# Last step of the experts: outputs and loads in column blocks, sums of the norm by block, and unread products

## The chip, the core and the metric

The kernel runs on one core of one Trainium2 chip. The metric is the time of one execution on the device in microseconds (us), the median over runs. PE is TensorE, PEld its weight loads, DVE is VectorE, ACT is ScalarE, POOL is GpSimd; SP issues the DMAs.

## What is computed

A transformer block, then a second block that ends in a mixture of 64 experts, for 256 tokens of width 1024, all in float32. What matters here is the end: each token goes through 6 of 64 experts, their weighted sum is added to the residual, and a norm over the 1024 outputs closes the block.

```python
def expert_block(xs):
    tok, g, e = xs
    xb = x_pad[tok]
    hb = jax.nn.silu(xb @ w_exp_gate[e]) * (xb @ w_exp_up[e])
    return (hb @ w_exp_down[e]) * g[:, None]
...
x = x + gate_f * moe_ffn(h, ...)
...
def rms_norm_2(x, gain):
    xf = x.astype(jnp.float32)
    y = xf * lax.rsqrt(jnp.mean(xf * xf, axis=-1, keepdims=True) + NORM_EPS)
    return (y * gain.astype(jnp.float32)).astype(x.dtype)
```

## The kernel before

The experts are sorted by load and worked off in 24 steps of 128 token slots each: steps of two experts with 64 slots or of four experts with 32 slots. The last step has four experts of 32 slots, so a product of one expert fills a quarter of the array's columns (128x32 weights) and one quarter of the partitions of its PSUM bank. Each expert brings three matrices of 1 MB: gate `eg` and up `eu` (1024x256) and down `ed` (256x1024). They are read once, so this part of the program is a long row of loads.

All loads are issued by SP in one order, set by `plan_step`; a load starts when a slot of SBUF is free, and up to eight are under way, since each waits for the landing of the one eight places earlier. In the last step `eu` comes in two halves of k and `ed` in two halves of output columns, `j` outside and experts inside.

A step runs so. `hidden(p)`: for gate and then up, k from 0 to 7 outside and experts inside, products accumulate in one bank; ACT and DVE make silu(gate) x up. `hidden_T` turns that around, `slots_T` makes `ST` (which slot belongs to which token) and `gcol` (the slots' gate weights). `down(p, c)`: for output half c, two k outside and experts inside, 32x512 products in one bank; DVE multiplies by `gcol` and `gate_f`; ACT and DVE split the result into `y_hi` and `y_lo`. `combine(p, c)` multiplies by `ST` and accumulates in four banks `moe[t][c]` (token half t, output half c) that hold the residual from the start (`seed`, where PE first runs four identity products over whole banks).

In the last step half 1 is not split: DVE leaves it as `yv` in float32. Then the norm. `half_norm` takes half 0: `measure` squares and sums a bank on ACT, `gained` multiplies it by the norm's gain on DVE. `norm` measures half 1, adds up, raises to the power -1/2 on POOL, scales (half 0 on ACT, half 1 on DVE) and stores four pieces of 128x512. PE, ACT and DVE work through their instructions in the order in which they are written; ACT and DVE wait for each other where both read one bank. Line numbers of the end:

```python
down(p, 0)
down(p, 1)
combine(p, 0)
half_norm()
combine(p, 1)
norm()
```

Of the kernel before, what the change touches and what calls it, by code (L numbers as in the profile page):

```python
# [10 lines left out]
F32 = mybir.dt.float32  # L11
# [4 lines left out]
OP = mybir.AluOpType  # L16
# [351 lines left out]
def tile_block(ctx: ExitStack, tc: tile.TileContext, a: dict, out: bass.AP, taps=None):  # L368
# [289 lines left out]
    steps = [step for g in groups for step in g]  # L658
    places = {}

    def plan_step(step, what, halves=1):
        r0, n_e, _ = step
        n = (D if what == "d" else KT) // halves

        def load(j, i):
            r = r0 + i
            if j == 0:
                experts[r, what] = b.slot([P, 2, D] if what == "d" else [P, KT, 256], F32, f"e{what}")
            src = {"g": w_eg, "u": w_eu, "d": w_ed}[what]
# [8 lines left out]
            part = (slice(None), slice(None), slice(j * n, (j + 1) * n)) if what == "d" else (slice(None), slice(j * n, (j + 1) * n))  # L678
            nc.sync.dma_start(t[part], src[part])
        for j in range(halves):  # L680
            for i in range(n_e):
                b.loads.append((lambda j=j, i=i: load(j, i), "ordered" if r0 + i >= FIXED else True))

    for u, step in enumerate(steps):
        if u == SH_AT:
            b.loads.append((lambda: y_sh.get(), True))
            sh_w = [plan_load([P, KT, 256], n, [(lambda t, n=n: t, rows(a[f"w_sh_{n}_2"][0], KT, True))], True) for n in ("gate", "up")]
        if u == SH_AT + 1:
            y_sh = b.lazy([P, 4, 512], F32, "y_sh")
            sh_d = plan_load([P, 2, D], "down", [(lambda t: t, rows(a["w_sh_down_2"][0], 2, True))], True)  # L690
        if u == len(steps) - 4:
            fin = b.lazy([P, 2, D], F32, "fin")
            b.loads.append((lambda: nc.sync.dma_start(fin[0:1, 0], a["g_final_2"].rearrange("(o n) -> o n", o=1)), True))
        for what in "gud":
            plan_step(step, what, 2 if u == len(steps) - 1 and what != "g" else 1)

    class Gemm:

# [1027 lines left out]
    def down(p, c):  # L1726
        r0, n_e, cap = steps[p]
        ps = b._bank(7 if c else p % 2)
        for k in range(2):
            for e in range(n_e):  # L1730
                r = slice(cap * e, cap * e + cap)
                nc.tensor.matmul(ps[r], hid[p][:, k, r], experts[r0 + e, "d"][:, k, c * 512:(c + 1) * 512], start=(k == 0), stop=(k == 1))  # L1732
        yv = b.slot([P, 512], F32, "yv") if p == NS - 1 and c == 1 else ps
        nc.vector.scalar_tensor_tensor(yv, ps, gcol[p], gate_f[:, c * 512:(c + 1) * 512], op0=OP.mult, op1=OP.mult)  # L1734
        if p == NS - 1 and c == 1:
            yhl[p, c] = yv,
            return
        y_hi, y_lo = b.tmp([P, 512], F32R, "y_hi"), b.tmp([P, 512], F32R, "y_lo")
        yhl[p, c] = y_hi, y_lo
        nc.scalar.copy(y_hi, yv)  # L1740
        nc.vector.tensor_tensor(y_lo, yv, y_hi.bitcast(F32), op=OP.subtract)  # L1741
        if c == 1:
            b.free(*(experts[r0 + e, "d"] for e in range(n_e)))
            b.pump()

    def combine(p, c):
        n = len(yhl[p, c])
        for i, part in enumerate(yhl[p, c]):
            for t in range(2):
# [63 lines left out]
    def hidden(p, between={}):  # L1813
# [71 lines left out]


    res = b.slot([P, 2, D], F32, "res")
    junk = b.slot([P, 512], F32, "junk")
    out_v = out[0].rearrange("(t p) d -> p t d", p=P)
    ss_rs = b.tmp([P, 3, 2], F32, "ss")  # L1890
    ss, rs = ss_rs[:, :2], ss_rs[:, 2]

    def measure(t, c):
        nc.scalar.activation(junk, moe[t][c], AF.Square, accum_out=ss[:, t, c:c + 1])

    def gained(t, c):
        cc = slice(c * 512, (c + 1) * 512)
        nc.vector.tensor_tensor(res[:, t, cc], moe[t][c], fin[:, 1, cc], op=OP.mult)

    def half_norm():  # L1900
        for t in range(2):
            measure(t, 0)
        for t in range(2):
            gained(t, 0)
        nc.vector.tensor_scalar(ss[:, :, 0], ss[:, :, 0], 1.0 / D, 1e-6, op0=OP.mult, op1=OP.add)

    def norm():
        for t in range(2):
            measure(t, 1)
            nc.vector.scalar_tensor_tensor(rs[:, t:t + 1], ss[:, t, 1:2], 1.0 / D, ss[:, t, 0:1], op0=OP.mult, op1=OP.add)  # L1910
            nc.gpsimd.tensor_tensor(rs[:, t:t + 1], rs[:, t:t + 1], b.neg_half[:, :1], op=OP.pow)
        for t in range(2):
            for c in range(2):
                d = res[:, t, c * 512:(c + 1) * 512]
                if c == 0:
                    nc.scalar.mul(d, d, rs[:, t:t + 1])
                else:
                    nc.vector.scalar_tensor_tensor(d, moe[t][c], rs[:, t:t + 1], fin[:, 1, 512:], op0=OP.mult, op1=OP.mult)
                nc.sync.dma_start(out_v[:, t, c * 512:(c + 1) * 512], d)
# [22 lines left out]
    with tc.If(count > 0):  # L1942
# [8 lines left out]
        with tc.For_i(0, NE, 1) as e:  # L1951
# [8 lines left out]
            for t in range(2):  # L1960
# [9 lines left out]
                for c in range(2):  # L1970
# [27 lines left out]
```

## Time and profile before

| what | us |
|---|---|
| median of 3 runs | 1041.77 |
| lowest and highest of them | 1039.08, 1043.4 |
| the profiled execution | 1040.18 |
| its span, first to last instruction | 1038.5 |
| PE busy in the span | 963.9 (93%) |
| DVE, ACT, POOL busy | 559.4, 410.9, 27.9 |

The page gives mean DMA traffic of 308 GB/s over the span; from the 23rd of 40 slices on, the experts, it is 383 to 422 GB/s in each but the last. A busy PE there is not a PE at its peak: it is counted busy while a product's record lasts. In the rows below a product in float32 has two records, one for each pass; "xN" counts records, and the time is from the first one's start to the last one's end. Records of products that follow each other overlap. What ended an engine's idle time stands in brackets.

### The profile page before, as it was taken

The numbers are of one execution on the slowest core, as the hardware profiler recorded it, in microseconds if no ns is written. First come the engines' busy times: TensorE is split into PE (matmuls) and PEld (weight loads), VectorE is DVE, ScalarE is ACT, GpSimd is POOL, SyncE is SP. The second block draws the span as 40 slices with busy tenths as digits, with TensorE's granted clock in tenths as the row PEclk, the third lists the DMA queues.
The fourth block names the chain that finished last, engine by engine and source line by source line (L and its number), as shares of the span: only waits on it lengthen the run. The fifth ranks groups of instructions, "written<-read, shape, count | busy, mean of one in ns | idle before, by whom it ended". The sixth has DMA issues, their size and how long they took to land.

```text
span 1038.5 us, 17524 instructions
## 1 busy us (share of the span) xinstructions
PE 963.9 (93%) x6844; PEld 723.2 (70%) x6844; DVE 559.4 (54%) x1193; ACT 410.9 (40%) x896; POOL 27.9 (3%) x88
## 2 busy tenths in 40 slices
PE   9999999999999899899999999999979997799776
PEld 7779889889977678798877566656635653456332
DVE  6986777788897865767877332223313231023112
ACT  5565666544455466464544221222212221112102
POOL 0000000100000110000000000000000000000000
PEclk9999999999999899899999999999989998899989
DMA  8976249383978236172897999999999999999995
GB/s 281 341 284 226 93 152 327 132 333 115 396 260 290 81 132 244 44 281 91 317 368 278 408 383 417 420 421 421 420 421 419 421 420 420 422 421 421 420 413 195
DMA packets 83455, 320.61 MB, mean 309 GB/s; under 512 B 10013, under 2 KB 12317, under 8 KB 56362
## 3 DMA queue, kind: packets, MB, share of 16 engines
q1 hardware_dynamic: 82482, 318.37, 78.6%
q8 instruction: 55, 0.90, 0.4%
q10 hardware_dynamic: 888, 1.09, 0.3%
q14 instruction: 30, 0.25, 0.1%
HBM read 318.37 MB, written 1.07 MB: 308 GB/s over the span
## 4 chain that ended last, share of the span: by engine, by line
DMA 34%; PE 20%; DVE 12%; ACT 4%; issue 1%; POOL 0%; SPq 0%; ACTq 0%; DVEq 0%; POOLq 0%
DMA eu<-in_w_exp_up_dram 12%; DMA ed<-in_w_exp_down_dram 11%; DMA eg<-in_w_exp_gate_dram 10%; PE bank L1824 4%; DVE lo L210 4%; PE bank L244 4%; PE bank L1732 3%; PE bank L242 2%; DVE mod_acc L589 1%; PE bank L1676 1%; PE bank L1751 1%; ACT hi L209 1%; PE bank L1283 1%; PE bank L1466 1%; DMA raw<-in_w_in_dram 1%
## 5 line engine op out<-in xcount | busy, mean ns | idle before, releaser
L210 DVE TENSOR_TENSOR lo<-raw,hi 128x512 fp32r<-128x512 f32 (+2 forms) x306 | 199.0, 689 | 50.7 <-ACT hi L209 48.3
L209 ACT CAST hi<-raw 128x512 fp32r<-128x512 f32 (+2 forms) x306 | 172.1, 618 | 55.3 <-DVE lo L210 23.3
L1824 PE MATMUL bank<-eu,xg 128*32 128x256 f32 (+1 forms) x1024 | 107.2, 417 | 22.1 <-DMA eu<-in_w_exp_up_dram 22.1
L1824 PE MATMUL bank<-eg,xg 128*32 128x256 f32 (+1 forms) x1024 | 100.6, 406 | 16.8 <-DMA eg<-in_w_exp_gate_dram 16.7
L1824 PEld LDWEIGHTS bank<-eu,xg 128*32 128x32 f32 (+1 forms) x1024 | 58.4, 133 | 65.7 <-DMA eu<-in_w_exp_up_dram 31.0
L1824 PEld LDWEIGHTS bank<-eg,xg 128*32 128x32 f32 (+1 forms) x1024 | 55.8, 130 | 66.6 <-DMA eg<-in_w_exp_gate_dram 22.6
L1830 DVE TENSOR_TENSOR hid<-bank,hid 128x256 f32<-128x256 f32 x24 | 10.2, 424 | 170.2 <-ACT hid L1829 170.2
L1732 PE MATMUL bank<-ed,hidT 128*64 128x512 f32 (+1 forms) x512 | 92.0, 597 | 1.4 <-ACT hidT L1724 0.7
L244 PE MATMUL bank<-hi,xTh 128*128 128x512 f32 x192 | 79.1, 412 | 4.6 <-DVE m L736 2.3
L1829 ACT ACTIVATE hid<-bank 128x256 f32<-128x256 f32 x24 | 9.2, 384 | 182.8 <-PE bank L1824 182.8
L244 PE MATMUL bank<-hi,xTl 128*128 128x512 f32 x192 | 75.9, 395 | 0.0
L244 PE MATMUL bank<-lo,xTh 128*128 128x512 f32 x192 | 75.0, 395 | 0.0
L242 PE MATMUL bank<-xTh,hi 128*128 128x256 f32 x256 | 73.7, 288 | 0.2 <-ACT ua L994 0.2
L242 PE MATMUL bank<-xTh,lo 128*128 128x256 f32 x256 | 72.5, 283 | 1.0 <-DVE lo L210 1.0
L242 PE MATMUL bank<-xTl,hi 128*128 128x256 f32 x256 | 72.4, 283 | 0.0
L1734 DVE SCALAR_TENSOR_TENSOR bank<-bank,gcol,gate_f 128x512 f32<-128x512 f32 x47 | 35.5, 755 | 51.3 <-PE bank L1732 51.3
L589 DVE SCALAR_TENSOR_TENSOR mod_acc<-wm,c_col,mod_acc 128x512 f32<-128x512 f32 x84 | 62.1, 746 | 0.0
L1740 ACT CAST y_hi<-bank 128x512 fp32r<-128x512 f32 x47 | 27.5, 585 | 85.2 <-DVE bank L1734 85.2
L1680 ACT ACTIVATE xg<-bank,mod_col,scale_f 128x256 f32<-128x256 f32 x88 | 44.8, 561 | 39.5 <-PE bank L1676 39.5
L1732 PEld LDWEIGHTS bank<-ed,hidT 128*64 128x64 f32 (+1 forms) x512 | 25.8, 123 | 48.9 <-issue 39.9
L1676 PE MATMUL bank<-S,xh_hi 128*128 128x256 f32 x176 | 49.0, 312 | 1.7 <-DVE y_lo L1741 1.0
L1741 DVE TENSOR_TENSOR y_lo<-bank,y_hi 128x512 fp32r<-128x512 f32 x47 | 32.5, 692 | 33.1 <-ACT y_hi L1740 33.1
(454 smaller groups left out, 1942.2 us busy)
## 6 DMA issues: line engine op xcount, KB each, us to landing
eg<-in_w_exp_gate_dram SPq DMA_DIRECT2D x64, 1024.0 KB, 19.7
eu<-in_w_exp_up_dram SPq DMA_DIRECT2D x60, 1024.0 KB, 19.7
ed<-in_w_exp_down_dram SPq DMA_DIRECT2D x60, 1024.0 KB, 19.7
raw<-in_w_in_dram SPq DMA_DIRECT2D x44, 1024.0 KB, 7.4
wm<-in_w_mod_dram SPq DMA_DIRECT2D x24, 1024.0 KB, 6.8
raw<-in_w_out_dram SPq DMA_DIRECT2D x8, 1024.0 KB, 10.1
raw<-in_w_in_dram SPq DMA_DIRECT2D x24, 256.0 KB, 4.8
raw<-in_w_branch_b_dram SPq DMA_DIRECT2D x4, 1024.0 KB, 5.8
```

The costliest lines, as they stand in the source:

```text
L209: nc.scalar.copy(slab.hi[:, k], slab.raw[:, k])
L210: nc.vector.tensor_tensor(slab.lo[:, k], slab.raw[:, k], slab.hi[:, k].bitcast(F32), op=OP.subtract)
L242: nc.tensor.matmul(ps, w[:, k, c0:c0 + n], act[a][:, k0 + k], start=(k0 == 0 and i == 0), stop=stop, skip_group_check=True)
L244: nc.tensor.matmul(ps, act[a][:, k0 + k, t * P:(t + 1) * P], w[:, k, c0:c0 + n], start=(k0 == 0 and left[o] == 3 * slab.kts - 1), stop=stop)
L589: nc.vector.scalar_tensor_tensor(d, r, c_col[:, k:k + 1], d, op0=OP.mult, op1=OP.add)
L1676: nc.tensor.matmul(ps[:, 256 * j:256 * j + 256], part[:, t, k + j], S[q][:, t], start=(j == 0 and n == 0), stop=(n == 3), skip_group_check ...
L1680: nc.scalar.activation(xg[q][:, k + j], ps[:, 256 * j:256 * j + 256], AF.Identity, scale=scale_f[:, k + j:k + j + 1], bias=shift_f[:, k + ...
L1732: nc.tensor.matmul(ps[r], hid[p][:, k, r], experts[r0 + e, "d"][:, k, c * 512:(c + 1) * 512], start=(k == 0), stop=(k == 1))
L1734: nc.vector.scalar_tensor_tensor(yv, ps, gcol[p], gate_f[:, c * 512:(c + 1) * 512], op0=OP.mult, op1=OP.mult)
L1740: nc.scalar.copy(y_hi, yv)
L1741: nc.vector.tensor_tensor(y_lo, yv, y_hi.bitcast(F32), op=OP.subtract)
L1824: nc.tensor.matmul(ps[r, 256 * c:256 * c + 256], xg[q][:, k, c0 + cap * e:c0 + cap * (e + 1)], experts[r0 + e, what][:, k], start=(k == 0 ...
```

## The change

The last step's `ed` is loaded in blocks of 512, 256 and 256 columns instead of two of 512 (`TAIL`); `eu` stays in two halves. Outputs 512 to 1023 are made by `last_out` in two blocks of 256 columns: experts outside and k inside, and after each expert but the last `stay_warm(2)`, two products of the identity in bf16, 128x512, into bank 2, which nobody reads. Each block has its own `yv` and its own `ST` products. The same unread pairs stand in the last step's `hidden` after experts 0 to 2, in gate at k 0 and in up at k 0 and k 4. `combine(p, 0)` moves behind the first of these blocks. The norm's sums are made for three blocks: `part_norm(0)`, `part_norm(1)`, and the last in `norm`. In `norm` columns 512 to 767, already multiplied by the gain, are scaled by an own instruction on DVE, and the stores stay four of 128x512.

```diff
-    def plan_step(step, what, halves=1):
+    def plan_step(step, what, last=False):
         r0, n_e, _ = step
-        n = (D if what == "d" else KT) // halves
+        full = D if what == "d" else KT
+        cuts = [0] + ({"g": [], "u": [4], "d": TAIL[:-1]}[what] if last else []) + [full]
...
+    def stay_warm(n):
+
+        ps = b._bank(2)
+        for _ in range(n):
+            nc.tensor.matmul(ps, ident16, ident16[:, None, :].to_broadcast([P, 4, P]), start=True, stop=True, skip_group_check=True)
+
+    def last_out(c0, c1, bank, yv):
+
+        p = NS - 1
+        r0, n_e, cap = steps[p]
+        n = c1 - c0
+        ps = b._bank(bank)
+        for e in range(n_e):
+            r = slice(cap * e, cap * e + cap)
+            for k in range(2):
+                nc.tensor.matmul(ps[r, :n], hid[p][:, k, r], experts[r0 + e, "d"][:, k, c0:c1], start=(k == 0), stop=(k == 1))
+            if e < n_e - 1:
+                stay_warm(2)
+        nc.vector.scalar_tensor_tensor(yv, ps[:, :n], gcol[p], gate_f[:, c0:c1], op0=OP.mult, op1=OP.mult)
+        for t in range(2):
+            nc.tensor.matmul(moe[t][1][:, c0 - 512:c1 - 512], ST[p][:, t * P:(t + 1) * P].bitcast(F32), yv, start=False, stop=True, skip_group_check=True)
...
+                    if p == NS - 1 and e < n_e - 1 and (k == 0 or c and k == 4):
+                        stay_warm(2)
...
-    def half_norm():
+    def part_norm(i):
+
         for t in range(2):
-            measure(t, 0)
+            measure(t, i)
         for t in range(2):
-            gained(t, 0)
+            gained(t, i)
...
     p = NS - 1
+    yv = b.slot([P, 512], F32, "yv")
     down(p, 0)
-    down(p, 1)
+    last_out(512, 768, 7, yv[:, :256])
     combine(p, 0)
-    half_norm()
-    combine(p, 1)
+    part_norm(0)
+    last_out(768, 1024, 0, yv[:, 256:])
+    part_norm(1)
     norm()
```

On PE, in the last step, the products of output columns 512 to 1023 and what follows stood like this before (bank 7 takes the products; the `ST` products go to the banks 3 to 6):

```order
L1732 MATMUL bank7_1409_9442<-ed_1379_9229,hidT_1399_9411 32x512
L1732 MATMUL bank7_1409_9442<-ed_1380_9231,hidT_1399_9411 32x512
L1732 MATMUL bank7_1409_9442<-ed_1381_9233,hidT_1399_9411 32x512
L1732 MATMUL bank7_1409_9442<-ed_1382_9235,hidT_1399_9411 32x512
...
L1751 MATMUL bank3_844_6117<-y_hi_1407_9438,ST_1401_9418 128x512
...
L1751 MATMUL bank5_846_6123<-y_lo_1408_9439,ST_1401_9418 128x512
L1751 MATMUL bank4_845_6120<-yv_1410_9451,ST_1401_9418 128x512
L1751 MATMUL bank6_847_6126<-yv_1410_9451,ST_1401_9418 128x512
```

The last block of the changed kernel, on the same engine, behind the `ST` products of outputs 0 to 511 (bank 0 takes the products of 256 columns, bank 2 the unread ones):

```order
L1749 MATMUL bank5_846_6123<-y_lo_1418_9471,ST_1410_9449 128x512
L1766 MATMUL bank0_1423_9504<-ed_1379_9229,hidT_1408_9442 32x256 x2
L1755 LDWEIGHTS ident16_82
L1755 MATMUL bank2_1424_9507<-ident16_82 128x512
L1755 LDWEIGHTS ident16_82
L1755 MATMUL bank2_1424_9507<-ident16_82 128x512
L1766 MATMUL bank0_1423_9504<-ed_1380_9231,hidT_1408_9442 32x256 x2
...
L1766 MATMUL bank0_1423_9504<-ed_1382_9235,hidT_1408_9442 32x256 x2
L1771 MATMUL bank4_845_6120<-yv_1415_9459,ST_1410_9449 128x256
L1771 MATMUL bank6_847_6126<-yv_1415_9459,ST_1410_9449 128x256
```

Four experts' products that stood side by side are now apart, each with its two k together, and whole-array products stand between them; the `ST` products of outputs 0 to 511 stand ahead of the last block.

On ACT the sums of squares of the norm stood like this before, one for each bank, then the scaling:

```order
L1894 ACTIVATE junk_1404_9426,ss_1405_9427<-bank5_846_6123 128x512 [waits PE_49,Activation_49]
L1894 ACTIVATE junk_1404_9426,ss_1405_9427<-bank4_845_6120 128x512 [waits PE_49,Activation_49]
L1894 ACTIVATE junk_1404_9426,ss_1405_9427<-bank6_847_6126 128x512 [waits PE_49,Activation_49]
L1916 ACTIVATE res_1403_9425<-res_1403_9425,ss_1405_9427 128x512 [waits DMAHW3_49,DMAHW5_49,DMAHW0_49,Pool_49]
```

And now, with what each waits for in brackets:

```order
L1921 ACTIVATE junk_1413_9457,ss_1414_9458<-bank5_846_6123 128x512 [waits PE_49]
L1921 ACTIVATE junk_1413_9457,ss_1414_9458<-bank4_845_6120 128x256 [waits PE_49,Activation_49]
L1921 ACTIVATE junk_1413_9457,ss_1414_9458<-bank6_847_6126 128x256 [waits PE_49,Activation_49]
L1921 ACTIVATE junk_1413_9457,ss_1414_9458<-bank4_845_6120 128x256 [waits DVE_49]
L1921 ACTIVATE junk_1413_9457,ss_1414_9458<-bank6_847_6126 128x256 [waits DVE_49]
L1945 ACTIVATE res_1412_9456<-res_1412_9456,ss_1414_9458 128x512 [waits DMAHW3_49,DMAHW5_49,DMAHW0_49,Pool_49]
```

The sums of banks 4 and 6 became two each. The first pair (columns 512 to 767) waits for PE, and the second pair (768 to 1023) waits for DVE alone: the wait for PE that the first pair made covers the last block's `ST` products, which write the same banks, and DVE's multiply of the middle block stands between the two pairs.

## Rows read from the trace of the kernel before

**Rows 1.** The page's head.
```profile
span 1038.5 us, 17524 instructions
```
**Rows 2.** The chain that ended last: start us, length us, what, from 1000 us.
```profile
1015.80 10.41 DMA ed<-in_w_exp_down_dram
...
1026.26 1.90 PE bank L1732 x10
...
1031.45 0.17 DVE ss L1910
...
1031.69 0.56 POOL ss L1911
```
**Rows 3.** PE by time, 1005 to 1031 us: start, length, engine, line, names, records.
```profile
1005.55 5.77 PE L1824 MATMUL bank<-eg,xg 128*32 128x256 f32 x57 [1.83 <-DMA eg<-in_w_exp_gate_dram]
...
1010.95 0.39 PE L1824 MATMUL bank<-eu,xg 128*32 128x256 f32 x3
...
1014.51 0.62 PE L1824 MATMUL bank<-eu,xg 128*32 128x256 f32 x2 [0.66 <-DMA eu<-in_w_exp_up_dram]
...
1015.83 1.91 PE L1824 MATMUL bank<-eu,xg 128*32 128x256 f32 x26 [0.70 <-DMA eu<-in_w_exp_up_dram]
...
1020.54 2.96 PE L1732 MATMUL bank<-ed,hidT 128*32 128x512 f32 x18 [0.37 <-ACT hidT L1724]
...
1023.73 1.04 PE L1732 MATMUL bank<-ed,hidT 128*32 128x512 f32 x2 [0.22 <-DMA ed<-in_w_exp_down_dram]
...
1024.98 1.05 PE L1732 MATMUL bank<-ed,hidT 128*32 128x512 f32 x2 [0.21 <-DMA ed<-in_w_exp_down_dram]
...
1026.26 1.90 PE L1732 MATMUL bank<-ed,hidT 128*32 128x512 f32 x10 [0.23 <-DMA ed<-in_w_exp_down_dram]
...
1028.66 0.62 PE L1751 MATMUL bank<-y_lo,ST 128*128 128x512 f32 x2
...
1029.12 1.88 PE L1751 MATMUL bank<-yv,ST 128*128 128x512 f32 x4
```
**Rows 4.** PE by time around `seed`, 578 to 580 us.
```profile
577.93 1.03 PE L1824 MATMUL bank<-eu,xg 128*64 128x256 f32 x8
578.89 1.04 PE L1783 MATMUL bank<-ident 128*128 128x512 bf16 x4
579.86 0.65 PE L1824 MATMUL bank<-eg,xg 128*64 128x256 f32 x4
```
**Rows 5.** Line 1783, `seed`: records' length in ns, shortest, median, longest.
```profile
L1783 PE MATMUL bank<-ident x4: 379/379/390, 578.9 to 579.6; 128*128 128x512 bf16 x4
```
**Rows 6.** Stretches: length, busy us (records) of PE, PEld, DVE, ACT, POOL; PE's granted clock, DMA.
```profile
1000.10:1003.50 3.40, 1.05 (x4) 0.28 (x4) 0.97 (x2) 0.58 (x1) 0.00 (x0) 1.00 1.01 411
1003.50:1006.90 3.40, 1.57 (x17) 0.66 (x20) 0.00 (x0) 0.00 (x0) 0.00 (x0) 0.50 1.03 411
1006.90:1010.30 3.40, 3.40 (x40) 1.56 (x36) 0.00 (x0) 0.00 (x0) 0.00 (x0) 0.50 1.00 389
...
1024.00:1027.40 3.40, 2.96 (x13) 0.51 (x12) 0.69 (x1) 0.54 (x1) 0.00 (x0) 1.00 0.12 45
```
**Rows 7.** Groups by form: busy us, mean ns of one, idle before.
```profile
L1830 DVE TENSOR_TENSOR hid<-bank,hid 128x256 f32<-128x256 f32 x24 | 10.2, 424 | 170.2 <-ACT hid L1829 170.2
...
L884 DVE SCALAR_TENSOR_TENSOR mixd<-pr,fac 128x256 f32<-128x256 f32 x8 | 3.8, 479 | 0.0
...
L1829 ACT ACTIVATE hid<-bank 128x256 f32<-128x256 f32 x24 | 9.2, 384 | 182.8 <-PE bank L1824 182.8
...
L1894 ACT ACTIVATION_READ_ACCUMULATOR junk<-bank 128x1 f32 x4 | 0.8, 194 | 0.0
```
**Rows 8.** DVE and SP by time in the tail.
```profile
1028.20 0.75 DVE L1734 SCALAR_TENSOR_TENSOR yv<-bank,gcol,gate_f 128x512 f32<-128x512 f32 x1 [2.94 <-PE bank L1732]
...
1033.02 1.83 SPq L1919 DMA_DIRECT2D out_dram<-res  x4
```
**Rows 9.** DMA issues of `ed` from 980 us: count, KB each, median us to landing.
```profile
ed<-in_w_exp_down_dram SPq DMA_DIRECT2D x8, 512.0 KB, 10.3
```

More of the change, by code (lines that the diff above doesn't have):

```diff
@@ L677, in load @@
             t = experts[r, what]
-            part = (slice(None), slice(None), slice(j * n, (j + 1) * n)) if what == "d" else (slice(None), slice(j * n, (j + 1) * n))
+            cut = slice(cuts[j], cuts[j + 1])
+            part = (slice(None), slice(None), cut) if what == "d" else (slice(None), cut)
             nc.sync.dma_start(t[part], src[part])
-        for j in range(halves):
+        for j in range(len(cuts) - 1):
             for i in range(n_e):
@@ L694, in tile_block @@
         for what in "gud":
-            plan_step(step, what, 2 if u == len(steps) - 1 and what != "g" else 1)
+            plan_step(step, what, u == len(steps) - 1)
     class Gemm:
@@ L1732, in down @@
                 nc.tensor.matmul(ps[r], hid[p][:, k, r], experts[r0 + e, "d"][:, k, c * 512:(c + 1) * 512], start=(k == 0), stop=(k == 1))
[L1733 to L1737, printed above, removed]
+        nc.vector.scalar_tensor_tensor(ps, ps, gcol[p], gate_f[:, c * 512:(c + 1) * 512], op0=OP.mult, op1=OP.mult)
+        yv = ps
         y_hi, y_lo = b.tmp([P, 512], F32R, "y_hi"), b.tmp([P, 512], F32R, "y_lo")
@@ L1746, in combine @@
     def combine(p, c):
-        n = len(yhl[p, c])
         for i, part in enumerate(yhl[p, c]):
             for t in range(2):
-                st = ST[p][:, t * P:(t + 1) * P]
-                nc.tensor.matmul(moe[t][c], st if n == 2 else st.bitcast(F32), part, start=False, stop=(p == NS - 1 and i == n - 1), skip_group_check=True)
+                nc.tensor.matmul(moe[t][c], ST[p][:, t * P:(t + 1) * P], part, start=False, stop=(p == NS - 1 and i == 1), skip_group_check=True)
+    def stay_warm(n):
[16 more added lines that the diff above has]
+            nc.tensor.matmul(moe[t][1][:, c0 - 512:c1 - 512], ST[p][:, t * P:(t + 1) * P].bitcast(F32), yv, start=False, stop=True, skip_group_check=True)
     select(0)
@@ L1900, in half_norm, with moe_block, measure, gained @@
-    def half_norm():
+    ss_rs = b.tmp([P, 2, 4], F32, "ss")
+    ss, rs = ss_rs[:, :, :3], ss_rs[:, :, 3]
+    blocks = [(0, 512)] + list(zip(TAIL, TAIL[1:]))
+    def moe_block(t, c0, c1):
+        return moe[t][c0 // 512][:, c0 % 512:c0 % 512 + c1 - c0]
+    def measure(t, i):
+        c0, c1 = blocks[i]
+        nc.scalar.activation(junk[:, t, :c1 - c0], moe_block(t, c0, c1), AF.Square, accum_out=ss[:, t, i:i + 1])
+    def gained(t, i):
+        c0, c1 = blocks[i]
+        nc.vector.tensor_tensor(res[:, t, c0:c1], moe_block(t, c0, c1), fin[:, 1, c0:c1], op=OP.mult)
@@ L1901, in half_norm @@
+    def part_norm(i):
         for t in range(2):
-            measure(t, 0)
+            measure(t, i)
         for t in range(2):
-            gained(t, 0)
-        nc.vector.tensor_scalar(ss[:, :, 0], ss[:, :, 0], 1.0 / D, 1e-6, op0=OP.mult, op1=OP.add)
+            gained(t, i)
+        if i == 0:
+            nc.vector.tensor_scalar(ss[:, :, 0], ss[:, :, 0], 1.0 / D, 1e-6, op0=OP.mult, op1=OP.add)
+        else:
+            nc.vector.scalar_tensor_tensor(ss[:, :, 0], ss[:, :, i], 1.0 / D, ss[:, :, 0], op0=OP.mult, op1=OP.add)
@@ L1907, in norm @@
     def norm():
+        c0, c1 = blocks[-1]
         for t in range(2):
[L1909 to L1910 removed]
+            measure(t, len(blocks) - 1)
+            nc.vector.scalar_tensor_tensor(rs[:, t:t + 1], ss[:, t, len(blocks) - 1:len(blocks)], 1.0 / D, ss[:, t, 0:1], op0=OP.mult, op1=OP.add)
             nc.gpsimd.tensor_tensor(rs[:, t:t + 1], rs[:, t:t + 1], b.neg_half[:, :1], op=OP.pow)
@@ L1912, in norm @@
         for t in range(2):
[L1913 to L1919, printed above, removed]
+            nc.scalar.mul(res[:, t, 0:512], res[:, t, 0:512], rs[:, t:t + 1])
```

17 lines of the change are left out of this document (8 added, 9 removed).

## The prediction

> **What bounds the kernel now.** I read the chain of waits first [rows 2]. Its last 50 us are loads: up to 1026.26 us each step waits for a piece of expert weights, the last being a 512-column half of `ed`. Behind that load stands a tail of 12.2 us, to the span's end at 1038.5 [rows 1, 2]: PE products (1.90), the second half's ST products, then square sums on ACT, a power on POOL at 1031.69, the scaling, and the stores. Next I read PE in order of time [rows 3]. In the last half PE waits for each piece: products start at 1023.73, 1024.98 and 1026.26, 1.26 apart, and one expert's 512-column product takes 1.04 of that. So PE is idle only 0.21 of 1.26 us there. That is the figure that matters: whatever is put between these products has little room.
>
> **The change, part by part. Loads.** The last `ed` half of each of four experts, 512 KB, becomes two loads of 256 KB; bytes and order stay. Pieces of 512 KB arrive 1.26 apart [rows 3]. A piece of half the size is not in the trace; it takes between 0.63 (half) and 1.26 (no gain from halving), so the last lands between 1026.26 and 1031.3 (four extra pieces of 1.26). I take 0.63 to 0.8, since such loads are fed eight deep (10.3 us from issue to landing, [rows 9]) and no wait for issue shows. The cost is nothing if PE comes to the last piece after that, which the next part shows; if that cover is gone, up to 5 us.
>
> **Products of a block.** Before, k runs outside and experts inside, and the four experts work side by side in quarters of the array: 13 products of 256 columns in 1.91 us, where a single one takes 0.62, hence 0.43 for each further product in the same quarter ((1.91 - 0.62) / 3) [rows 3]. In `last_out` the expert runs outside: two products of one expert in one quarter, 0.62 + 0.43 = 1.05, then two unread products over the whole array, then the next expert. What that pattern costs stands once in the trace, at `seed` [rows 4]: quarter or half-array products end at 577.93 + 1.03 = 578.96, four identity products of 128x512 in bf16 follow (1.04 in all, 0.38 for one record [rows 5], so 0.22 from one to the next), and products of an expert start again at 579.86. That is 0.90 from the end of the records to the next product for four, 0.90 - 2 x 0.22 = 0.46 for two. One expert step is 1.05 + 0.46 = 1.51 us, and a block of four 3 x 1.51 + 1.05 = 5.6 us, against 2.5 to 3.2 us in which its pieces land. So both blocks are bound by PE, not by loads. Bounds for the two unread products with their changes of form are 0 (if they ran beside the quarters) and 0.90 (as long as four). I take 0.46, from the nearest row.
>
> The row shows 0.24 of changes of form per pair beyond the streaming (0.46 - 0.22). The Trainium skill, "TensorEngine Tiling (Array Packing)", section Tiling Modes, Key Properties, says that changing the tiling mode drains TensorE; it speaks against this change. With a whole drain each way (0.38 - 0.22 = 0.16, twice) the two blocks would come out 0.5 later than by the row; the sum goes by the row.
>
> **Unread products in `hidden`.** The last step gets them after experts 0 to 2 in gate k 0 and in up k 0 and k 4. In gate they fall into waits of 1.8 us and are hidden. In up each step is 0.62 + 0.46 = 1.08 where four products took 0.43 together. If PE ran at 2.4 GHz through gate, gate's eight rows end at 1005.55 + 8 x 0.43 = 1008.99 (the arrival of its last piece, [rows 3]); up k 0 reaches expert 3 at + 3 x 1.08 = 1012.2, three more rows give 1013.5, and k 4 reaches expert 3 at 1016.8, against 1015.83 [rows 3]: 0.9 late, carried to all that follows. But the clock in 1003.5 to 1010.3 is 0.50, 1.2 GHz, after a stretch in which PE was busy 1.05 of 3.40 us [rows 6], and gate's rows then ended at 1010.95 [rows 3]. If it stays so, up starts 2.0 later and the lateness is 2.9. That is the second case below.
>
> The unread products add some 0.9 of work to each 2.5 us of that wait. The Trainium skill, "TensorE: Matmul & The Clock Gate", Part 1, says that half rate is the default and that activity releases it; by that rule the change gives the first case, 0.9. No row shows PE with such a mixture, so the other stays open.
>
> **Tail.** Now the chain, at 0.9 late. Outputs 0 to 511 start at 1020.54 + 0.93 = 1021.47 and take two rows of 0.86 (1.04 for one product of two passes, [rows 3], less its 0.18 of tail). Block 512 to 767 starts at 1023.2, ends at 1028.8. DVE scales it: 0.48 for 256 columns [rows 7], 1029.3. Its two ST products start 0.17 later, as yv's did (1028.20 + 0.75 to 1029.12, [rows 3, 8]), and take 0.43 each: 1030.35. Behind them on PE's queue stand the four ST products of outputs 0 to 511, 0.23 each (1028.66 to 1029.12 for two, [rows 3]): 1031.3. Then the last block, 1031.4 to 1037.0, DVE to 1037.5, and the ST product of tokens 0 to 127 ends at 1038.26. ACT and DVE do block 0's sums beside the last block; that is the gain the change has. But the middle block's sums stand behind the last block's ST products in the program, and on one PSUM bank ACT and DVE take turns (ACT, DVE, ACT). From 1038.34 ACT squares two middle blocks, 0.48 each (0.38 + 0.19 less 0.1 of overlap, [rows 7]); DVE multiplies each for 0.42 after it, to 1039.27 and 1039.76; ACT's first last-block sum runs 1039.36 to 1039.84; DVE's two small sums of 0.17 [rows 2] end at 1040.11; POOL starts at 1040.19. Before, POOL started at 1031.69 [rows 2]. What follows is the same: ACT scales 512 columns, SP issues the first store when that ends and the next three 0.47 apart ([rows 8]: 1.83 for four), and the store's own lines wait for nothing else; DVE's extra 256-column multiply ends before SP comes to its store. So the end moves by 1040.19 - 1031.69 = 8.5 us.
>
> **The time.** The profiled execution took 1040.18 (span 1038.5 and 1.7 around it), the median of the three runs is 1041.77. The sum gives 1048.7 against the first, 1050.3 against the second; I take the median's, 1050.
>
> **Rivals.**
> First, the clock still falls in gate's waits: another 2.0, so + 10.5, 1052. For it: the fall at 1003.5 stands in the trace [rows 6] and the added work is small. Against: the added work is as large again as what was there.
> Second, not slower: the unread products and changes of form cost nothing beside the landing of pieces. Then PE is done with expert 2 when the last piece lands at 1026.26, and the tail is 1.05 (two products of 256 columns), 0.52 for DVE, 0.17, 0.6, and 1.93 from there to POOL as above: 1030.5, 1.2 before 1031.69, 1040.6. It decides at an expert step of 0.63 to 0.8 us, the landing of a piece; two products of one expert alone take 1.05 or, overlapped with the next expert's, 0.43. Against it is the seed's row [rows 4], in which nothing ran beside the identity products.
> Third, the unread products cost their streaming alone, no change of form: 6 steps of 1.29, + 7.2, 1049. It lies within the range.
> Fourth, the clock falls in the tail itself and the two blocks double: + 11 more, 1061. Against it: 1.00 at 1024 to 1027.4, with PE busy 2.96 of 3.40 [rows 6], and PE would be busier now.
>
> **How the numbers follow.** First case (8.5) 0.47, clock still low (10.5) 0.30, streaming alone (7.2) 0.09, the last in the tail 0.03, nothing beside the landings (- 1.2) 0.07, something in between, 2 to 5 us, 0.04. A measurement of this kernel can tell about 0.5%, 5.2 us, from no change. The first four lie over it, less some noise: slower 0.86, same 0.12, faster 0.02. The runs before spread over 4 us, so 1.5 us go on either side: the range is 1046 to 1054, which holds the first three cases.
>
> **What would show it.** Right: in the changed trace expert steps of `last_out` start about 1.5 us apart with no wait for `ed`, the last block ends near 1037, POOL's power starts near 1040. Wrong: PE waits for `ed` in the last block, or steps come 0.6 to 0.8 apart; the up products of k 4 end as before; the clock column shows 0.50 in 1003 to 1010 (then the first rival). If block sums of the middle run while PE is still in the last block, I have misread the order, and 1.0 us is gained back.

## The result

The changed kernel takes 1049.77 us (median of 9 runs, 1045.18 to 1052.21), the kernel before 1040.14 in the runs beside it (9 runs): ratio 1.0093, 95% interval 1.008 to 1.0105, so 9.6 us slower. The profiled execution took 1048.84, its span is 1047.1 (before 1038.5, [rows 1]). A second measurement beside other runs gave 1046.65, ratio 1.0065 (1.0049 to 1.008); why the two differ is told with the experiments.

| what | before | after |
|---|---|---|
| median, us | 1040.14 | 1049.77 |
| span of the profiled execution | 1038.5 | 1047.1 |
| PE busy | 963.9 | 973.4 |
| POOL's power starts | 1031.69 | 1040.29 |

First PE in order of time, the rows that answer to [rows 3] (cuts are marked by dots): start, length, engine, line, names, records, and in brackets the idle time ahead and what ended it.

```profile
1004.46 5.05 PE L1844 MATMUL bank<-eg,xg 128*32 128x256 f32 x57 [1.83 <-DMA eg<-in_w_exp_gate_dram]
...
1010.20 0.62 PE L1844 MATMUL bank<-eu,xg 128*32 128x256 f32 x2
...
1011.28 0.62 PE L1844 MATMUL bank<-eu,xg 128*32 128x256 f32 x2
...
1021.63 1.92 PE L1735 MATMUL bank<-ed,hidT 128*32 128x512 f32 x16 [0.37 <-ACT hidT L1727]
1023.37 1.03 PE L1766 MATMUL bank<-ed,hidT 128*32 128x256 f32 x4
1024.33 0.61 PE L1755 MATMUL bank<-ident 128*128 128x512 bf16 x2
1024.87 1.05 PE L1766 MATMUL bank<-ed,hidT 128*32 128x256 f32 x4
...
1026.39 1.05 PE L1766 MATMUL bank<-ed,hidT 128*32 128x256 f32 x4
...
1027.91 1.05 PE L1766 MATMUL bank<-ed,hidT 128*32 128x256 f32 x4
1029.54 1.13 PE L1771 MATMUL bank<-yv,ST 128*128 128x256 f32 x4 [0.58 <-DVE yv L1769]
...
1031.52 1.05 PE L1766 MATMUL bank<-ed,hidT 128*32 128x256 f32 x4
...
1036.07 1.05 PE L1766 MATMUL bank<-ed,hidT 128*32 128x256 f32 x4
1037.70 1.13 PE L1771 MATMUL bank<-yv,ST 128*128 128x256 f32 x4 [0.58 <-DVE yv L1769]
```

No row behind 1021.63 waits for `ed`. Experts start 1.50 to 1.52 apart, and a block takes 5.59 us (1023.37 to 1028.96) and 5.60 (1031.52 to 1037.12). What follows the last products, all engines in order of time:

```profile
1037.16 0.48 DVE L1769 SCALAR_TENSOR_TENSOR yv<-bank,gcol,gate_f 128x256 f32<-128x256 f32 x1 [3.63 <-PE bank L1766]
...
1038.50 0.38 ACT L1921 ACTIVATE junk<-bank 128x256 f32<-128x256 f32 x1 [5.78 <-PE bank L1771]
...
1039.01 0.86 DVE L1925 TENSOR_TENSOR res<-bank,fin 128x256 f32<-128x256 f32 x2 [1.36 <-ACT junk L1921]
...
1039.46 0.38 ACT L1921 ACTIVATE junk<-bank 128x256 f32<-128x256 f32 x1
...
1040.29 1.07 POOL L1943 TENSOR_TENSOR ss<-ss,neg_half 128x1 f32<-128x1 f32 x2 [72.85 <-DVE ss L1942]
```

The rows at 1038.50 and 1039.01 belong to the middle block: its sums begin only behind the last block's `ST` products, and the last block's own first sum is the row at 1039.46. From the end of the products, 1037.12, to the power 3.17 us pass.

Last the stretches that answer to [rows 6], columns as there; PE's granted clock is the last figure but two:

```profile
1000.10:1003.50 3.40, 1.86 (x4) 0.27 (x4) 0.00 (x0) 0.00 (x0) 0.00 (x0) 0.63 1.02 406
1003.50:1006.90 3.40, 2.44 (x24) 1.18 (x28) 0.00 (x0) 0.00 (x0) 0.00 (x0) 0.50 1.03 405
1006.90:1010.30 3.40, 3.40 (x43) 1.44 (x36) 0.00 (x0) 0.00 (x0) 0.00 (x0) 0.87 0.98 384
```

The clock fell here too, one stretch sooner than before, and came back sooner (0.50, then a mean of 0.87): PE ran gate's long row at 1.2 GHz (0.50) for the most part of its time and at 2.4 GHz at its end.

### The profile page after: what moved, and what is told of

It is laid out like the page before. It is cut to its first block, busy times and chain, and to the rows that moved or that the text cites. A ratio compares the mean times of both kernels' runs of the same rounds, so it can differ in the third digit from the quotient of the medians.

```text
span 1047.1 us, 17645 instructions
## 1 busy us (share of the span) xinstructions
PE 973.4 (93%) x6894; PEld 724.7 (69%) x6894; DVE 560.3 (54%) x1199; ACT 411.5 (39%) x900; POOL 27.8 (3%) x88
## 3 DMA queue, kind: packets, MB, share of 16 engines
q10 hardware_dynamic: 888, 1.09, 0.3%
## 4 chain that ended last, share of the span: by engine, by line
PE 35%; DMA 18%; DVE 12%; ACT 5%; issue 1%; POOL 0%; ACTq 0%; DVEq 0%; SPq 0%; POOLq 0%
PE bank L1844 11%; DMA eu<-in_w_exp_up_dram 8%; DMA ed<-in_w_exp_down_dram 6%; PE bank L1735 5%; DVE lo L211 4%; DMA eg<-in_w_exp_gate_dram 4%; PE bank L245 4%; PE bank L1679 3%; PE bank L1749 3%; PE bank L243 2%; DVE mod_acc L590 1%; PE bank L1469 1%; ACT hi L210 1%; PE bank L1766 1%; PE bank L1286 1%
## 5 line engine op out<-in xcount | busy, mean ns | idle before, releaser
L1844 PE MATMUL bank<-eg,xg 128*32 128x256 f32 (+1 forms) x1024 | 104.6, 420 | 18.1 <-DMA eg<-in_w_exp_gate_dram 18.1
L1844 PE MATMUL bank<-eu,xg 128*32 128x256 f32 (+1 forms) x1024 | 104.5, 411 | 16.3 <-DMA eu<-in_w_exp_up_dram 16.3
L1735 PE MATMUL bank<-ed,hidT 128*64 128x512 f32 (+1 forms) x496 | 87.8, 597 | 1.6 <-DMA ed<-in_w_exp_down_dram 0.9
L243 PEld LDWEIGHTS bank<-xTh,lo 128*128 128x128 f32 x256 | 49.1, 192 | 1.8 <-DVE lo L211 1.8
```

The lines of the kernel that those rows point to most:

```text
L243: nc.tensor.matmul(ps, w[:, k, c0:c0 + n], act[a][:, k0 + k], start=(k0 == 0 and i == 0), stop=stop, skip_group_check=True)
```

## The experiments

Two lengths put all profiles side by side. **A** runs from the start of gate's long row (the last `eg` piece is there; the row with x57 above) to the start of the last step's outputs (first row with `ed`); **B** from there to the start of POOL's power. The last `eg` piece comes at 1004.46 to 1009.40 in the profiles, and A and B leave that out; A keeps the waits for `eu` (in the run without unread products they make it 15.72). After the power nothing differs: about 6.8 us follow it in each. A profile is one execution and the ratio comes from several. B repeats within 0.06 us between executions of one kernel, A does not, so A + B less that of before can lie off the timed difference, here by up to 2 us; what B shows is firm, an A is a sample. The clock is the mean granted clock of the stretches, as in [rows 6], that gate's long row lies in. In the changed kernel A is 1021.63 - 1004.46 = 17.17 and B 1040.29 - 1021.63 = 18.66; before, A is 1020.54 - 1005.55 = 14.99 and B 11.15 [rows 2, 3].

| kernel | ratio to before, 95% interval | A | B | clock in gate's long row |
|---|---|---|---|---|
| before | 1 | 14.99 | 11.15 | 0.50 |
| changed | 1.0093 (1.008 to 1.0105) | 17.17 | 18.66 | 0.50, then 0.87 |
| changed, again | 1.0065 (1.0049 to 1.008) | 15.57 | 18.66 | 1.00 |
| no unread products | 1.001 (0.9999 to 1.0021) | 15.72 | 12.15 | 0.50 |
| none in `hidden` | 1.0082 (1.006 to 1.0105) | 17.73 | 18.67 | 0.50, then 0.60 |
| none in `hidden`, again | 1.0064 (1.0049 to 1.0078) | 14.96 | 18.66 | 0.50 |
| none in `last_out` | 1.0032 (1.0021 to 1.0042) | 16.04 | 11.62 | 0.51, then 1.00 |
| before, with those of `hidden` | 1.0003 (0.9994 to 1.0012) | 17.64 | 8.54 | 0.50 |
| four instead of two | 1.0111 (1.0091 to 1.0132) | 17.92 | 21.26 | 0.50 |
| six ahead of each block | 1.0035 (1.0022 to 1.0048) | 17.24 | 12.59 | 0.55 |
| in quarters | 1.0037 (1.0023 to 1.0051) | 17.88 | 13.93 | 0.50, then 0.65 |
| sums ahead | 1.0077 (1.0053 to 1.0102) | 17.25 | 17.57 | 0.58 |
| reordered | 0.9985 (0.9971 to 0.9999) | 14.92 | 9.77 | 0.50 |
| reordered, again | 0.9984 (0.9973 to 0.9994) | 15.07 | 9.83 | 0.50 |

**No unread products at all.**

```diff
-            if e < n_e - 1:
-                stay_warm(2)
...
-                    if p == NS - 1 and e < n_e - 1 and (k == 0 or c and k == 4):
-                        stay_warm(2)
```

> The changed kernel without any unread product: blocks of 512, 256 and 256 columns, cut loads and block sums stay; what is read from the output is the same. Theory A (the unread products and their changes of form carry the loss, the blocks themselves carry none): experts of a block overlap in their quarters, a block of four takes about 5 x 0.43 = 2.2 us, so PE comes to the last piece of 256 KB as it lands; behind it the tail is 1.05 us of products and 3.15 us to POOL's power (after: 1037.14 to 1040.29), 1.2 us shorter than before: ratio to before about 0.999 (0.997 to 1.000). Theory B (the order with the expert outside, the smaller loads or the additional sums carry the loss): PE waits for `ed` in the last block and the power starts 5 us or more later than before, ratio 1.005 or more. Theory C (the loss stands in `hidden`, by lateness and clock): also about 0.999 here; the next two tell A from C.

Measured: 1.001. Nearly the whole loss goes with the unread products, so theory B (the blocks themselves carry it) falls. But the 1.2 us that the blocks were to win are not there either: B is 12.15, 1.00 longer than before. All engines in order of time:

```profile
1025.28 0.69 DVE L1741 TENSOR_TENSOR y_lo<-bank,y_hi 128x512 fp32r<-128x512 f32 x1 [0.71 <-ACT y_hi L1740]
...
1025.89 0.47 DVE L1767 SCALAR_TENSOR_TENSOR yv<-bank,gcol,gate_f 128x256 f32<-128x256 f32 x1
...
1026.41 1.13 PE L1769 MATMUL bank<-yv,ST 128*128 128x256 f32 x4 [0.82 <-DVE yv L1767]
...
1028.41 1.09 PE L1766 MATMUL bank<-ed,hidT 128*32 128x256 f32 x16
...
1029.05 1.29 DVE L1921 TENSOR_TENSOR res<-bank,fin 128x512 f32<-128x512 f32 x2 [2.69 <-ACT junk L1917]
...
1030.32 0.48 DVE L1767 SCALAR_TENSOR_TENSOR yv<-bank,gcol,gate_f 128x256 f32<-128x256 f32 x1
...
1033.44 1.07 POOL L1939 TENSOR_TENSOR ss<-ss,neg_half 128x1 f32<-128x1 f32 x2 [63.76 <-DVE ss L1938]
```

The last block's sixteen passes start at 1028.41, directly behind `ST` products and without a wait for `ed`. These `ST` products waited 0.82 us for `yv` of the middle block, which stands behind `y_lo` on DVE. And the last block, done at 1029.50, is scaled only at 1030.32, since the gain of outputs 0 to 511 stands ahead of it on DVE. So the chain begins at the outputs 0 to 511, not at the last piece. The row at 1028.41 also tells what a block costs undisturbed: 1.09 us for four experts, against 5.6.

**None in `hidden`, none in `last_out`, those of `hidden` alone.** The first two take one of the two pieces above out of the changed kernel; the third adds the second piece to the kernel before.

> The changed kernel without the unread products in `hidden`; those in `last_out` stay. Theory A: blocks stay bound by PE at 1.51 us for an expert step; up's steps fall from 1.08 to 0.43 us, so the last step's outputs start 0.9 to 2.2 us sooner after the last `eu` piece: ratio to before 1.007 to 1.0085 (1047.5 to 1049), against 1.0093 of the changed kernel. Theory B: no change from the changed kernel's 1.0093 by more than 0.1%. Theory C: ratio about 1.000 to 1.002.

> The changed kernel without the unread products in `last_out`; those in `hidden` stay. Theory A: blocks take about 2.2 us, PE starts the outputs 1 to 2 us late but waits for the last piece of `ed` all the same, so the lateness is absorbed: ratio to before 0.998 to 1.001. Theory B: 1.005 or more. Theory C: 1.007 or more, with the lateness of up seen in the time of the last block.

> The kernel before with the unread products of `hidden` alone (18 of 128x512 in bf16 in the last step). Theory A: up ends 1 to 2 us late, but the outputs then find their pieces there and catch up before the last piece of `ed` lands (before, PE waited 0.37 + 0.22 + 0.21 + 0.23 us among the last outputs and ran 0.86 us for a row): ratio to before 1.000 (0.999 to 1.0015). Theory C: 1.005 or more. If the clock falls by one stretch more or less in gate's waits, it shows in the granted clock between 1000 and 1010 us, with up to 2 us more of lateness, of which at most 1 us reaches the end.

Measured: 1.0082, 1.0032, 1.0003. Without those in `last_out` 6 of the 9.6 us are gone by the first measurement of the changed kernel, 3.5 of 6.9 by the second, and B is 7.04 shorter, so theory C falls. PE and POOL by time:

```profile
1021.87 1.92 PE L1735 MATMUL bank<-ed,hidT 128*32 128x512 f32 x16 [0.37 <-ACT hidT L1727]
1023.61 1.52 PE L1766 MATMUL bank<-ed,hidT 128*32 128x256 f32 x16
...
1028.46 1.09 PE L1766 MATMUL bank<-ed,hidT 128*32 128x256 f32 x16
...
1033.49 1.07 POOL L1941 TENSOR_TENSOR ss<-ss,neg_half 128x1 f32<-128x1 f32 x2 [63.57 <-DVE ss L1940]
```

The third came as expected, and its rows show the absorption:

```profile
1005.94 5.50 PE L1830 MATMUL bank<-eg,xg 128*32 128x256 f32 x57 [0.47 <-DMA eg<-in_w_exp_gate_dram]
...
1023.58 2.87 PE L1732 MATMUL bank<-ed,hidT 128*32 128x512 f32 x22 [0.38 <-ACT hidT L1724]
1026.68 1.91 PE L1732 MATMUL bank<-ed,hidT 128*32 128x512 f32 x10 [0.23 <-DMA ed<-in_w_exp_down_dram]
```

The outputs start 2.65 us later than before behind gate (A 17.64), run without the first two waits for `ed` of [rows 3] and are back at the last piece, where PE waits again: B is 2.61 shorter. For 1.0032 my expectation (0.998 to 1.001) was wrong by the same step as above: in the changed kernel's order the outputs' start is the head of the chain, with or without unread products, so lateness is not absorbed. A is 1.05 longer than before and B 0.47, 1.5 us in that profile; timed it is 3.3 (2.2 to 4.4). The rest is not in that profile and stays open: there the clock came back after one stretch of gate, and whether other executions had a longer A no run shows.

The first left open what `hidden` costs: 1.0082 against 1.0093, and its profile has a long A of 17.73. That execution is one of two of the six that took longer (1049.74 and 1053.68; the others 1046.03 to 1046.57). Here the clock fell a second time, in up's waits: gate and up of this kernel, PE in order of time, and a stretch as in [rows 6]:

```profile
1004.74 5.81 PE L1844 MATMUL bank<-eg,xg 128*32 128x256 f32 x57 [1.86 <-DMA eg<-in_w_exp_gate_dram]
...
1016.11 3.35 PE L1844 MATMUL bank<-eu,xg 128*32 128x256 f32 x26 [0.67 <-DMA eu<-in_w_exp_up_dram]
...
1017.10:1020.50 3.40, 3.40 (x22) 1.77 (x15) 0.42 (x1) 0.38 (x1) 0.00 (x0) 0.60 0.89 312
```

The row of 26 records took 3.35 us where before it took 1.91 [rows 3], and the granted clock has a mean of 0.60 there. So both kernels were run again side by side.

> The changed kernel itself beside the next run on the same chip: 1.0093 (1.008 to 1.0105). Its profile shows whether the last `eg` piece lands 1.1 us sooner than before in it by chance (then near 1005.5 here) and in which stretch of gate the granted clock is 0.50.

> The changed kernel without the unread products in `hidden`, beside the changed kernel on the same chip. Theory A: 1 to 2 us below it, ratio to before 1.007 to 1.0085. Rival (the unread products keep the clock up in the waits of up, and what they cost there they give back): equal, 1.009 or more, with a granted clock of 0.50 in a stretch of up.

Measured: 1.0065 and 1.0064. Both lie under what I expected: the changed kernel did not repeat its 1.0093, and the other is not 1 to 2 us below it. The two are equal, as the rival had it, but not for its reason: the kernel without those products shows 0.50 in gate and no fall in up. This time the changed kernel's profile has the clock up through gate:

```profile
1004.89 3.42 PE L1844 MATMUL bank<-eg,xg 128*32 128x256 f32 x57 [1.36 <-DMA eg<-in_w_exp_gate_dram]
...
1020.46 1.99 PE L1735 MATMUL bank<-ed,hidT 128*32 128x512 f32 x16 [0.37 <-ACT hidT L1727]
...
1039.12 1.07 POOL L1943 TENSOR_TENSOR ss<-ss,neg_half 128x1 f32<-128x1 f32 x2 [70.17 <-DVE ss L1942]
...
1003.50:1006.90 3.40, 2.04 (x41) 1.24 (x44) 0.00 (x0) 0.00 (x0) 0.00 (x0) 1.00 1.00 396
1006.90:1010.30 3.40, 3.40 (x35) 1.22 (x28) 0.00 (x0) 0.00 (x0) 0.00 (x0) 1.00 1.03 409
```

Its A is 15.57, 0.58 longer than before, and without those in `hidden` A is 14.96. The unread products of `hidden` thus cost 0.6 us where the clock stays up, 2.2 where it falls in gate as in the first profile, and 2.65 to 2.93 in three runs in which it stayed low longer (the kernel before with those of `hidden`, the quarters, the four); without them a fall in gate costs nothing, since PE waits for `eu` afterwards all the same, and a fall in up costs 2.7. Neither the one kernel nor the other is measurably better (1.0065 and 1.0064). Which of the cases an execution meets no run here can set. The first measurement of the changed kernel fits A + B of its profile (2.18 + 7.51 = 9.7 us, measured 9.6), the second the other case (0.58 + 7.51 = 8.1, measured 6.9, interval 5.1 to 8.3). That the two cases make the difference between the measurements is argued from one profile of each, not shown execution by execution.

**What of the pairs costs: number, place, form.** Four instead of two; the same twelve, but six ahead of each block; the same twelve in the quarter of the expert just done:

```diff
-                stay_warm(2)
+                stay_warm(4)
```
```diff
         ps = b._bank(bank)
+        stay_warm(6)
...
-            if e < n_e - 1:
-                stay_warm(2)
```
```diff
-                stay_warm(2)
+                warm = b._bank(2)
+                for _ in range(2):
+                    nc.tensor.matmul(warm[r], ident16[:, :cap], ident16[:, None, :].to_broadcast([P, 4, P]), start=True, stop=True, skip_group_check=True)
```

> The changed kernel with four unread products instead of two behind each of the experts 0 to 2 in `last_out`. Theory A (the steps stand on the path, so each additional product is paid in full): an expert step of 1.52 us becomes 1.52 + 2 x 0.22 = 1.95, six steps, + 2.6 us: ratio to before about 1.0118 (1.011 to 1.013). Rival D (only the change of form between quarters and the whole array is paid, the streaming lies beside the next expert's loads or waits): steps stay at 1.52, ratio 1.009.

> The changed kernel with the same twelve unread products in `last_out`, but six ahead of each block instead of two behind each of the experts 0 to 2; the four experts' products follow each other. Theory A (what is paid is above all that a whole-array product between two experts keeps their quarters from running side by side, and the changes of form): a block takes 6 x 0.22 + 0.2 + 1.1 = 2.6 us (1.1 us for sixteen passes stood in the run without tail products) instead of 5.6; PE's end comes 5 to 6 us sooner, down to what the queues leave: ratio to before 1.0033 to 1.005. Rival (the streaming of the twelve products carries the loss): no change, 1.008 to 1.010.

> The changed kernel, its unread products in `last_out` with weights of 128x32 instead of 128x128, in the quarter of the expert just done; as many products and columns as before. Theory A (what is paid is that a product over the whole array waits for the quarter ahead of it and holds up the quarter behind it): the next expert's quarter starts beside the unread products, a block takes 1.1 + 0.43 = 1.5 to 2.5 us instead of 5.6, ratio to before 1.003 to 1.005, as with the six together. Rival (streaming of additional products costs by itself, wherever they stand): 1.05 + 0.43 = 1.48 us for a step less the changes of form of 0.2, so 1.29, blocks of 4.9 us, ratio 1.0075 to 1.009.

Measured: 1.0111, 1.0035, 1.0037. With four, PE by time:

```profile
1024.99 1.03 PE L1766 MATMUL bank<-ed,hidT 128*32 128x256 f32 x4
1025.95 1.04 PE L1755 MATMUL bank<-ident 128*128 128x512 bf16 x4
1026.92 1.05 PE L1766 MATMUL bank<-ed,hidT 128*32 128x256 f32 x4
...
1028.87 1.05 PE L1766 MATMUL bank<-ed,hidT 128*32 128x256 f32 x4
```

Steps of 1.93 to 1.95, 0.43 more for two products, and B is 2.60 longer: six steps of 0.43, each paid in full. With six together:

```profile
1028.50 1.47 PE L1755 MATMUL bank<-ident 128*128 128x512 bf16 x6
1029.89 1.09 PE L1767 MATMUL bank<-ed,hidT 128*32 128x256 f32 x16
1031.62 1.13 PE L1770 MATMUL bank<-yv,ST 128*128 128x256 f32 x4 [0.64 <-DVE yv L1768]
```

As many unread products, yet a block takes 2.48 us instead of 5.59: the four experts run side by side again. Against the kernel with none in `last_out` (B 11.62) the twelve products cost 7.04 between the experts, 0.97 ahead of the blocks (where part of them falls into PE's wait for `yv`), and 2.31 in quarters. The rival that the streaming of the twelve products carries the loss falls. In quarters a block took 3.2 us (1024.16 to 1027.37), more than the 2.5 I had allowed.

**The middle block's sums ahead of the last block.**

```diff
-    last_out(768, 1024, 0, yv[:, 256:])
     part_norm(1)
+    last_out(768, 1024, 0, yv[:, 256:])
     norm()
```

> The changed kernel with the sums of squares and the gain of columns 512 to 767 emitted ahead of the last block instead of behind it. Theory A: ACT and DVE do them beside the last block's products; from the end of these products to POOL's power 2.1 us pass instead of 3.15: - 1.0 us, ratio to before about 1.0083 (1.0073 to 1.0093). Rival: the last block's `ST` products now wait for these reads of their banks, or ACT's second pair stands elsewhere on the path, and nothing is won: 1.0093, 3.1 us from the products' end to the power.

Measured: 1.0077; the interval (1.0053 to 1.0102) alone doesn't tell 1 us. The profile does: B is 17.57, 1.09 shorter. ACT now has the middle block's sums beside the last block's products, and one sum of each token half behind them:

```profile
1033.93 0.38 ACT L1921 ACTIVATE junk<-bank 128x256 f32<-128x256 f32 x1
...
1039.77 0.39 ACT L1921 ACTIVATE junk<-bank 128x256 f32<-128x256 f32 x1 [5.00 <-PE bank L1771]
...
1040.52 1.07 POOL L1943 TENSOR_TENSOR ss<-ss,neg_half 128x1 f32<-128x1 f32 x2 [72.03 <-DVE ss L1942]
```

The last products end at 1038.45, the power starts 2.07 later instead of 3.17.

**Reordered, without unread products.** The `ST` products of a small block become a function of their own, `last_combine`; columns 512 to 1023 are gained and scaled from the banks in one operation, as before the change.

```diff
     last_out(512, 768, 7, yv[:, :256])
     combine(p, 0)
+    last_out(768, 1024, 0, yv[:, 256:])
+    last_combine(512, 768, yv[:, :256])
     part_norm(0)
-    last_out(768, 1024, 0, yv[:, 256:])
     part_norm(1)
+    last_combine(768, 1024, yv[:, 256:])
     norm()
```

> Without any unread product, blocks of 512, 256 and 256 columns and cut loads as in the changed kernel, and another order: PE does the products of both small blocks before the `ST` products of the first of them; DVE scales both blocks before it takes up block 0's gain; the middle block's sums stand ahead of the last block's `ST` products; columns 512 to 1023 are gained and scaled in one operation at the end. Theory: in the run without unread products PE came to the last block only at 1028.41, behind `ST` products that waited for DVE, 1.8 us after its last piece had landed, and DVE scaled it 0.9 us late behind block 0's gain. With the order mended the last products end 1.1 us behind the last piece, the power starts about 3.3 us behind it (before: 5.4): ratio to before 0.998 (0.9970 to 0.9995). Rival (the landing of the smaller loads or the chain of outputs 0 to 511 through DVE and ACT decides): 1.000 to 1.0015.

> The reordered kernel without unread products a second time, on another chip if it falls so: 0.9985 (0.997 to 1.000) if the gain of about 1.5 us is one; 1.000 or more if it was the chip.

Measured: 0.9985 and 0.9984, so about 1.6 us faster than the kernel before, twice. All engines by time in the first:

```profile
1025.46 0.73 PE L1749 MATMUL bank<-y_hi,ST 128*128 128x512 f32 x2
...
1026.62 1.61 PE L1766 MATMUL bank<-ed,hidT 128*32 128x256 f32 x16
...
1028.27 0.48 DVE L1767 SCALAR_TENSOR_TENSOR yv<-bank,gcol,gate_f 128x256 f32<-128x256 f32 x1 [1.98 <-PE bank L1766]
1028.67 1.28 DVE L1923 TENSOR_TENSOR res<-bank,fin 128x512 f32<-128x512 f32 x2
...
1031.00 1.07 POOL L1941 TENSOR_TENSOR ss<-ss,neg_half 128x1 f32<-128x1 f32 x2 [60.57 <-DVE ss L1940]
```

The last block starts 1.8 us sooner than in the run without unread products (the outputs of both start within 0.06 of each other, 1021.23 and 1021.29), DVE scales it 0.04 us behind its end (1028.23), and the power comes 2.77 behind that. B is 1.38 shorter than before. Within its row of sixteen records three experts start together at 1026.62 and the fourth only at 1027.18, which fits the landing of the last piece there, though the row names no wait. From 1027.18 to the power it is 3.8 us (expected 3.3); before, from the products of the last piece, it was 5.4 (1026.26 to 1031.69 [rows 2, 3]).

## Why the prediction was right, point by point

The prediction was 1050 in 1046 to 1054, slower by over 0.5%; measured 1049.77. The signs of being right that it named are there; of its signs of being wrong one is there too, a clock of 0.50 between 1003 and 1010.

That the time came within 0.3 us is luck in part. The base was the median of three runs, 1041.77, and nine runs gave 1040.14, 1.6 less; the sum of 8.5 was 1.1 less than the 9.6 measured. The two errors offset each other. Both measurements of the changed kernel lie in the range.

| step | forecast | measured |
|---|---|---|
| expert step in `last_out` | 1.51 | 1.50 to 1.52 |
| from the records' end to the next expert | 0.46 | 1024.87 - 1024.40 = 0.47 |
| block of four | 5.6 | 5.59, 5.60 |
| a step of up with its pair | 1.08 | 1.08 (1010.20 to 1011.28) |
| outputs 0 to 511 start | 1021.47 | 1021.63 |
| last block | 1031.4 to 1037.0 | 1031.52 to 1037.12 |
| from outputs' start to the power (B) | 1040.19 - 1021.47 = 18.72 | 18.66 in both profiles |

**Products of a block and their price.** The price read at `seed` [rows 4] was that of the new pattern. What was only argued, that the pairs stand on PE's path, the runs showed: twice as many cost 2.60 us more, and without them B falls by 7.04. A block of 5.6 us against 1.09 undisturbed is made of three parts: streaming of the pairs 3 x 0.43 = 1.3, 3 x (1.52 - 2 x 0.43 - 0.43) = 0.7 that is left over and is put down to the changes of form, and 3 x 0.86 = 2.6 because the experts' two products each follow one another instead of running side by side (1.09 + 4.6 = 5.7). The third and largest part is in the forecast's 1.05 + 0.46, but I had not called it by name. Without the pairs the two blocks take 1.52 and 1.09, 8.6 us less together; 7.04 of it reach the end, since PE then waits 1.34 and 1.36 us for `yv` instead of 0.58 each time. The Trainium skill, "TensorEngine Tiling (Array Packing)", Tiling Modes, Key Properties, says that a change of tiling mode drains TensorE; the trace agrees that the changes cost, 0.23 us for a pair, both ways; a whole drain each way, as the prediction reckoned it, would be 0.32. Products in quarters, which need no such change and leave the other quarters running beside them, cost a third. The prediction's own figure of 0.24 for a pair was worked out wrongly, since 0.46 - 0.22 takes off one product of the two and leaves out the record's tail; 1.51 - 0.86 - 2 x 0.22 gives 0.21. The sum does not use it, only the comparison with a whole drain does.

**Loads.** Hidden, as forecast: no row of the last two blocks waits for `ed`. What the smaller loads cost by themselves is read from the reordered kernel, if the fourth expert's start is taken for the landing of the last piece: the fourth expert of the last block starts 20.87 us behind the start of gate's long row (1006.31 to 1027.18), in the second profile 21.08 (1005.34 to 1026.42). Before, with pieces of 512 KB, it was 20.71 (1005.55 to 1026.26). So the last piece came 0.2 to 0.4 us later, near the lower end of the prediction's bounds.

**`hidden` and the clock.** This step failed. The first case, 0.9 us late at full clock, was given 0.47, the first rival (clock still low, 2.9) 0.30. In the profile the clock was 0.50 in gate, the rival's sign, and A was 2.18 longer; the full 2.9 is what the quarters and the four show (2.89, 2.93). That the outputs nevertheless started at 1021.63, where 1021.47 was forecast, is chance: in that execution the last `eg` piece was there 1.09 sooner (1004.46 against 1005.55). The sum with 2.18 in place of 0.93 is 8.5 + 1.25 = 9.75, and the median moved by 9.6. In the second measurement's profile the clock stayed up, A was 0.58 longer, and the sum with that is 8.15 (measured 6.9, 5.1 to 8.3). That it is 0.58 and not 0.93 is a count: behind the last `eg` piece there stand 58 records of gate (57 in the long row and one more), so 7.25 rows of four products and not the eight of the sum, 0.32 us less. So both cases occur, and the prediction should have given them as two times of one kernel and not as rivals of which one is true. The Trainium skill, "TensorE: Matmul & The Clock Gate", Part 1, says that the throttled state is the default and that activity releases the throttle. By that rule the change was to give the first case. The profile of the second measurement agrees (1.00 through gate), that of the first does not (0.50); the unread products did not make sure of it.

**Tail.** B is right within 0.1 us, also where the forecast spoke of the middle block's sums: it put 1.0 on their place behind the last `ST` products, and moving them gave 1.09.

**The second rival** (not slower, - 1.2, were the pairs free) had the wrong size: without any pair the ratio is 1.001 (0.9999 to 1.0021). Its tail was counted from the last piece, but in the changed order the `ST` products of the middle block stand ahead of the last block on PE, and the gain of block 0 ahead of `yv` on DVE. Had the pairs been free, the kernel would have been no faster. The third rival (streaming alone, steps of 1.29) is refuted by the steps of 1.50 to 1.52, the fourth (clock low in the tail) by the same steps and a granted clock of 1.00 there.

## What to carry to other kernels

A product over the whole array between products that work in quarters costs more than its own columns: it ends the running side by side, so read the price from the gap in which such a pattern already stands, and put such work ahead of the group, not into it. Cutting the last step finer shortens a tail only if the queues are cut with it: what waits for the last block must not stand behind another block's work on PE, DVE or ACT. To see a microsecond in a kernel whose loads wander by more, measure from an event that the change can't move, and take more than one profile where the clock can fall.

## What the runs showed of the hardware that was not expected

Sixteen passes of four experts in four quarters, data at hand, took 1.09 us from the first one's start to the last one's end; one expert's four passes alone take 1.03 to 1.05. Expert outside and k inside, I had counted 2.2 us for it; yet four records start in the first 0.05 us of that row. They are one of each expert, since one expert's passes start 0.22 apart ((1.05 - 0.38) / 3), although in the program each expert's four passes stand together.

The same program, the changed kernel, had a granted clock of 0.50 through most of gate's row in one execution and of 1.00 in the other. Ahead of it PE was busy 2.60 of 4.10 us (996.0 to 1000.1) where the clock then fell, and 3.70 of 4.10 where it stayed up: the same instructions, but the pieces of the step before lay differently in time. That share alone does not sort the runs: in the kernel before with those of `hidden` PE was busy for all 4.10 us there, and the clock fell to 0.50 behind it all the same. All six profiles of kernels without unread products in `hidden` have 0.50 in gate, and one of them a second fall in up, with 3.35 us for a row of 1.91; of the eight with them one had 1.00 all through gate. The unread products did not make sure of the clock, and whether they changed the chance no run here measures.
